# A two-layer diffusion trunk on one core: another order of two modulation sums, and another engine for their first products

## The chip, the cores and the metric

The kernel runs on one core of a Trainium2 chip. The metric is the device time of one execution in microseconds. The kernel before took 1355.4 us (median of three runs, 1355.3 to 1356.14). The profiled execution took 1356.77 us, of which 1355.0 us lie between its first and its last recorded instruction.

## What is computed

Two layers run over 384 tokens (128 context tokens, 256 latent tokens) of width 2048. What matters here is the modulation that each layer draws from two condition vectors (`c_ctx` for context tokens, `c` for latent ones):

```
for layer in range(2):
    m = silu(cond) @ w_mod + b_mod            # cond: c_ctx and c; w_mod 2048 x 6144
    shift, scale, gate = split(m, 3)          # columns 0-2047, 2048-4095, 4096-6143
    h = rmsnorm(x, norm_g) * (1 + scale) + shift
    x = x + gate * mixer(h)                   # mixer: projections, attention, output projection
```

All numbers are float32. The `gate` columns of layer 0 are needed when layer 0's output projection is added to x. The `shift` and `scale` columns of layer 1 are needed when layer 1's input is made out of that sum.

## The kernel before, in words

**The matrix work.** Every projection is cut into groups of 512 output columns (`group`, line 375). A group loads its weights in eight pieces of 512 KB (`w_piece`, line 365) through the DMA queue of SyncE. ScalarE rounds each piece to a short format (`whi`, line 370), VectorE makes the rest (`wlo`, line 372), and TensorE makes three products for each tile. The results stand in PSUM banks with the tag `mm`, of which there are four; a group in the token-major form uses three of them. Three `whi` and two `wlo` buffers exist. Weight pieces are issued with a high priority, everything else in the order in which the program emits it. A scheduler then orders each engine's instructions once, ahead of the run; on the chip each engine and each DMA queue works strictly in that order.

**The modulation sums.** Of layer 0 the scale and shift columns are made by TensorE in the first 215 us (`start_mod`). All others come from eight sums on VectorE, each over 1024 columns of a `w_mod` (`mod_acc`, line 263): for each of 16 row blocks a piece of 512 KB is loaded on SyncE's queue into one of three `mraw` buffers, and for each of the two condition vectors the piece, times a scalar per partition, is added to `acc`. `acc` has one buffer: the next sum can't write it before the sum ahead has been read out. A unit of such a sum is one row block (two instructions). The first row block has no sum yet to add to, and is a plain product (line 284).

**The two ends of a sum.** `mod_part` (line 291) ends with four small TensorE matmuls that add over partitions, a ScalarE copy `ev` (line 300), four transposes, and one or two small VectorE instructions: it gives shift or scale columns of layer 1. `mod_gates` (line 311) first waits, while the program is written, until a flag says that the tiles it writes are free (line 314); its end then broadcasts `b_mod` by DMA on GpSimd's queue, splits `acc` into `ahi` (ScalarE) and `alo` (VectorE) four times, adds over partitions by eight matmuls, and adds the bias four times on VectorE. It gives two groups of gate rows.

**Who decides when.** The sums stand in two lists, `mods` and `rows` (line 336); `unit` (line 338) runs the next unit, `rows` ahead of `mods`, one sum at a time. `pump` (line 348) is called after each weight piece. It runs units while the pace allows and while the planned VectorE time, plus 2.7, stays under the planned TensorE time (lines 350 to 354). Planned times are added up by `cost_v` and `cost_t` (lines 56 to 66) for VectorE and TensorE instructions only; a lead of TensorE beyond 6.0 is dropped. `finish` (line 356) runs units at once until the gate rows that are needed exist. It is called after each group of layer 0's output projection (line 1076), before its three PSUM tiles are multiplied by the gate rows.

**The order of the sums.** `mods` holds layer 1's columns from blocks 16, 24, 0 and 8, and then the first gate rows of layer 0 (line 776). The flag of the latter, `ready0`, is set at line 1032, after the last group but one ahead of the output projection. The gate rows for the third and fourth group go into `rows` after the first group (line 1079). `finish_mods` (line 1084) empties `mods` before the fourth group is used.

Of the kernel before, what the change touches and what calls it, by code (L numbers as in the profile page):

```python
# [10 lines left out]
AF = mybir.ActivationFunctionType  # L11
ALU = mybir.AluOpType
# [33 lines left out]
def trunk_kernel(ctx: ExitStack, tc: tile.TileContext, I, O):  # L46
# [39 lines left out]
    nc = Core()  # L86
# [15 lines left out]
    def nm(s):  # L102
        uid[0] += 1
        return f"{s}_{uid[0]}"

    def px():
        return psx.tile([P, 512], F32, tag="px", name=nm("px"))

    def t6(tag, dt=F32):
        return tpool.tile([P, 1536], dt, tag=f"t{tag}", name=nm(f"t{tag}"))  # L110
# [138 lines left out]
    def mod_cols(l, k0, nk, cp):  # L249

        like = (lambda a: a.rearrange("p (h b) c -> p h b c", h=2)) if len(cp.shape) == 4 else (lambda a: a)
        nc.vector.tensor_tensor(
            out=like(modc[l][:, k0:k0 + nk, :]), in0=cp,
            in1=like(bcol[l][:, k0:k0 + nk].unsqueeze(2).broadcast_to([P, nk, 2])), op=ALU.add)
        if KT <= k0 < 2 * KT:
            q = slice(k0 - KT, k0 - KT + nk)
            nc.vector.scalar_tensor_tensor(
                out=acol[l][:, q, :], in0=modc[l][:, k0:k0 + nk, :], scalar=1.0,
                in1=gcol[l][:, q].unsqueeze(2).broadcast_to([P, nk, 2]), op0=ALU.add, op1=ALU.mult)
# [3 lines left out]
    def mod_acc(l, c0):  # L263

        acc = mpool.tile([P, 2, 1024], F32, tag="acc", name=nm("acc"))
        cs = csil_g[l] if c0 >= 2 * D else csil
        raws = []

        def load(kt):
            raws.append(wpool.tile([P, 1024], F32, tag="mraw", bufs=MRAWB, name=nm("mraw")))  # L270
            nc.sync.dma_start(raws[kt], I[f"l{l}_w_mod"][kt * P:kt * P + P, c0:c0 + 1024])


        for kt in range(MRAWB - 1):
            load(kt)
        yield
        for kt in range(KT):
            if kt + MRAWB <= KT:
                load(kt + MRAWB - 1)
            raw = raws[kt]  # L280
            for c in range(2):
                s = cs[:, kt, c:c + 1]
                if kt == 0:
                    nc.vector.tensor_scalar(out=acc[:, c], in0=raw, scalar1=s, scalar2=None, op0=ALU.mult)
                else:
                    nc.vector.scalar_tensor_tensor(out=acc[:, c], in0=raw, scalar=s, in1=acc[:, c],
                                                   op0=ALU.mult, op1=ALU.add)
            yield
        return acc

    def mod_part(l, k0):

        acc = yield from mod_acc(l, k0 * P)
        ps = px()
        for j in range(4):
            nc.tensor.matmul(ps[32 * j:32 * j + 32, :], lhsT=ones[:, 0:32],
                             rhs=acc[:, j % 2, 512 * (j // 2):512 * (j // 2) + 512], start=True, stop=True)
        ev = mpool.tile([P, 512], F32, tag="t2", bufs=T2B, name=nm("ev"))
        with tc.high_priority(BOOST):
            nc.scalar.copy(ev, ps)  # L300
        for _ in range(EVY):
            yield
        cp = px()
        for b in range(4):
            nc.tensor.transpose(cp[:, b * P:b * P + P], ev[:, b * P:b * P + P], ident)
        mod_cols(l, k0, 8, cp.rearrange("p (b h c r) -> p h b c r", b=4, h=2, c=2)[:, :, :, :, 0])
        yield
# [3 lines left out]
    def mod_gates(l, g0, tags, ready):  # L311

        acc = yield from mod_acc(l, 2 * D + 512 * g0)
        while not ready[0]:
            yield
        for i in range(2):
            c0 = 2 * D + 512 * (g0 + i)
            gb = t6(tags[i])[:, 0:1024].rearrange("p (c n) -> p c n", c=2)
            for c in range(2):
                nc.gpsimd.dma_start(gb[:, c], I[f"l{l}_b_mod"][c0:c0 + 512].partition_broadcast(P))  # L320
            for c in range(2):
                ps = px()
                a = acc[:, c, 512 * i:512 * i + 512]
                hi = mpool.tile([P, 512], F32R, tag="t2", bufs=T2B, name=nm("ahi"))
                nc.scalar.copy(hi, a)
                lo = mpool.tile([P, 512], F32R, tag="t2", bufs=T2B, name=nm("alo"))
                nc.vector.tensor_tensor(out=lo, in0=a, in1=hi.bitcast(F32), op=ALU.subtract)
                nc.tensor.matmul(ps, lhsT=ones_r, rhs=hi, start=True, stop=False)
                nc.tensor.matmul(ps, lhsT=ones_r, rhs=lo, start=False, stop=True)
                nc.vector.tensor_tensor(out=gb[:, c], in0=ps, in1=gb[:, c], op=ALU.add)  # L330
            gates[l, g0 + i] = gb
        yield
# [3 lines left out]
    mods, rows, now = [], [], []  # L336
# [436 lines left out]

    phases = START
    ready0 = [False]
    mods += [mod_part(1, k0) for k0 in (16, 24, 0, 8)] + [mod_gates(0, 0, "KL", ready0)]
    pace[1] = RATE0
    for _ in start_mod(*phases[0]):
        pass
# [452 lines left out]
def _program(shapes):  # L1232
    import concourse.bacc as _bacc

    nc = _bacc.Bacc("TRN2", target_bir_lowering=False, num_devices=1)
    I = {n: nc.dram_tensor(f"in_{n}_dram", s, d, kind="ExternalInput").ap() for n, (s, d) in shapes.items()}
    O = {n: nc.dram_tensor(f"out_{i}_dram", s, F32, kind="ExternalOutput").ap() for i, (n, s) in enumerate(_OUTS)}
    with tile.TileContext(nc) as tc:
        trunk_kernel(tc, I, O)
    return nc  # L1240
# [12 lines left out]
```

## Time and profile before

| | us |
|---|---|
| median of three runs | 1355.4 |
| the profiled execution | 1356.77 |
| its span, first to last instruction | 1355.0 |
| TensorE matmul busy | 1321.0 (97%) |
| VectorE busy | 1019.0 (75%) |
| ScalarE busy | 647.9 (48%) |
| GpSimd busy | 72.4 (5%) |

PE stands for TensorE's matmuls, PEld for its weight loads, DVE for VectorE, ACT for ScalarE, POOL for GpSimd, SP for SyncE. Line 77 is a helper through which every VectorE and TensorE instruction goes, so these are told apart by tile names: `mm` is a result of a weight group, `px` any other PSUM tile, `acc` and `mraw` belong to the modulation sums. Neighbouring matmuls overlap in the records, so that a busy TensorE says that its queue was not waiting, not that it did more than one thing. In the timeline, the number in brackets at the end of a line is how long the engine stood idle before, and what ended that.

### The profile page before, as it was taken

To read this page: it belongs to the slowest core of one execution; us is meant where nothing else is said; L and a number is where in the kernel's file an instruction comes from. 1 tells how busy PE (TensorE), PEld (TensorE's weight loads), DVE (VectorE), ACT (ScalarE), POOL (GpSimd) and SP (SyncE) were. 2 spreads that over 40 slices of the span, in tenths; PEclk is the share of its full clock that TensorE was granted. 3 is DMA by queue.
4 is the path that set the end of the run, shared out by engine and by line. 5 is a ranking of instruction groups with operands and counts; after the bars stand their busy time and mean duration, and the time that the engine had idled before them with its cause. 6 is when DMAs were issued, how large, how long until landed. Compare 5 with 4: busy or idle time off the path is not lost.

```text
span 1355.0 us, 19101 instructions
## 1 busy us (share of the span) xinstructions
PE 1321.0 (97%) x7093; PEld 1125.7 (83%) x7093; DVE 1019.0 (75%) x1602; ACT 647.9 (48%) x1297; POOL 72.4 (5%) x84
## 2 busy tenths in 40 slices
PE   5899999999999999999999999999999999999998
PEld 4678888997888878787987887888888999998887
DVE  5678757998998745896998969995656664499743
ACT  4532233476655534755433347345766763352221
POOL 1000000000000021101000000200000101000000
PEclk8899999999999999999999999999999999999999
DMA  9989989755555334576778854784332345457642
GB/s 284 304 289 331 317 289 319 236 160 179 176 174 181 97 106 138 167 232 201 242 244 254 297 184 133 234 283 119 92 94 81 104 118 166 129 181 254 210 152 84
DMA packets 138317, 265.42 MB, mean 196 GB/s; under 512 B 8944, under 2 KB 46768, under 8 KB 138224
## 3 DMA queue, kind: packets, MB, share of 16 engines
q1 hardware_dynamic: 132592, 246.52, 56.9%
q0 software_dynamic: 5376, 17.60, 4.5%
q8 instruction: 56, 0.92, 0.3%
q14 instruction: 37, 0.30, 0.1%
q10 hardware_dynamic: 256, 0.08, 0.0%
HBM read 256.04 MB, written 8.13 MB: 195 GB/s over the span
## 4 chain that ended last, share of the span: by engine, by line
PE 91%; DMA 4%; DVE 3%; ACT 1%; POOL 1%; issue 0%; DVEq 0%; ACTq 0%; SPq 0%; POOLq 0%
PE mm L77 77%; PE px L77 14%; DMA raw<-in_l_w_in_dram 2%; DMA mraw<-in_l_w_mod_dram 1%; DVE wlo L77 1%; DVE acc L77 1%; DMA tB<-in_x_sample_dram 0%; ACT whi L370 0%; POOL sm L444 0%; DVE tB L77 0%; DMA rowc<-in_c_dram 0%; DVE tG L77 0%; ACT tE L469 0%; DVE tH L77 0%; POOL r L444 0%
## 5 line engine op out<-in xcount | busy, mean ns | idle before, releaser
L370 ACT CAST whi<-raw 128x1024 fp32r<-128x1024 f32 (+1 forms) x270 | 278.4, 1032 | 500.1 <-PE mm L77 393.7
L77 DVE TENSOR_TENSOR wlo<-raw,whi 128x1024 fp32r<-128x1024 f32 (+1 forms) x270 | 323.4, 1198 | 188.0 <-PE mm L77 148.6
L77 PE MATMUL mm<-whi,hh 128*128 128x512 f32 x1008 | 398.9, 396 | 0.0
L77 PE MATMUL mm<-wlo,hh 128*128 128x512 f32 x1008 | 391.7, 391 | 3.2 <-DVE wlo L77 3.2
L77 PE MATMUL mm<-whi,hl 128*128 128x512 f32 x1008 | 393.5, 391 | 0.6 <-DVE hl L77 0.6
L77 DVE SCALAR_TENSOR_TENSOR acc<-mraw,csil,acc 128x1024 f32<-128x1024 f32 x240 | 299.0, 1279 | 9.0 <-DMA mraw<-in_l_w_mod_dram 9.0
L77 PE MATMUL mm<-hh,whi 128*128 128x384 f32 x768 | 264.4, 347 | 7.1 <-ACT hh L471 4.6
L77 PE MATMUL mm<-hl,whi 128*128 128x384 f32 x768 | 259.2, 338 | 0.0
L77 PE MATMUL mm<-hh,wlo 128*128 128x384 f32 x768 | 254.5, 338 | 0.2 <-DVE wlo L77 0.2
L77 PEld LDWEIGHTS mm<-wlo,hh 128*128 128x128 f32 x1008 | 189.3, 188 | 42.7 <-DVE wlo L77 5.8
L77 PEld LDWEIGHTS mm<-whi,hl 128*128 128x128 f32 x1008 | 189.3, 188 | 40.8 <-DVE hl L77 1.5
L77 PEld LDWEIGHTS mm<-whi,hh 128*128 128x128 f32 x1008 | 189.4, 188 | 39.3 <-ACT tE L824 0.8
L77 PEld LDWEIGHTS mm<-hh,whi 128*128 128x128 f32 x768 | 145.3, 190 | 22.2 <-issue 10.1
L77 PEld LDWEIGHTS mm<-hh,wlo 128*128 128x128 f32 x768 | 144.8, 189 | 2.7 <-DVE wlo L77 1.0
L77 PEld LDWEIGHTS mm<-hl,whi 128*128 128x128 f32 x768 | 145.5, 190 | 1.2 <-issue 0.2
L623 ACT ACTIVATE p<-px,nb,rs 128x384 f32<-128x384 f32 (+1 forms) x72 | 42.4, 596 | 15.0 <-DVE nb L77 14.5
L77 PE MATMUL px<-mraw,cs 128*32 128x256 f32 (+1 forms) x576 | 40.4, 377 | 4.9 <-DMA mraw<-in_l_w_mod_dram 4.9
L633 ACT ACTIVATE p<-p,sum 128x384 f32<-128x384 f32 (+1 forms) x72 | 36.1, 540 | 15.1 <-DVE sum L77 13.2
L77 DVE TENSOR_REDUCE mx<-px 128x1 f32<-128x384 f32 (+1 forms) x54 | 29.7, 567 | 9.3 <-PE px L77 8.9
L77 PEld LDWEIGHTS px<-mraw,cs 128*32 128x32 f32 x576 | 16.3, 114 | 20.0 <-issue 8.2
L77 PEld LDWEIGHTS px<-ct,p 128*128 128x128 f32 x168 | 20.1, 141 | 8.3 <-issue 2.8
L444 POOL TENSOR_TENSOR rs<-rs,nhalf 128x12 f32<-128x12 f32 x6 | 14.7, 2450 | 227.5 <-DVE rs L77 227.5
(415 smaller groups left out, 1228.5 us busy)
## 6 DMA issues: line engine op xcount, KB each, us to landing
raw<-in_l_w_in_dram SPq DMA_DIRECT2D x194, 512.0 KB, 3.9
mraw<-in_l_w_mod_dram SPq DMA_DIRECT2D x192, 512.0 KB, 5.0
raw<-in_l_w_out_dram SPq DMA_DIRECT2D x64, 512.0 KB, 4.9
raw<-in_l_w_in_dram SPq DMA_DIRECT2D x12, 256.0 KB, 6.6
tK<-in_l_b_mod_dram POOLq DMA_DIRECT2D x6, 256.0 KB, 6.0
y1d<-tA POOLq DMA_DIRECT2D x2, 768.0 KB, 5.2
tD<-y1d POOLq DMA_DIRECT2D x2, 768.0 KB, 6.0
tL<-y1d POOLq DMA_DIRECT2D x2, 768.0 KB, 6.2
```

Source lines behind the costliest of these rows:

```text
L77: return f(*a, **k)
L370: nc.scalar.copy(hi, raw)
L444: nc.gpsimd.tensor_tensor(out=out, in0=out, in1=nhalf[:, 0:out.shape[1]], op=ALU.pow)
L623: nc.scalar.activation(p[:, j], ss[j], AF.Exp, bias=nb[:, j:j + 1], scale=rs[:, i + j:i + j + 1], accum_out=sm[:, j:j + 1])
L633: nc.scalar.activation(p[:, j], p[:, j], AF.Copy, scale=sm[:, j:j + 1])
```

## The change

```
 mod_acc, line 281:
             for c in range(2):
                 s = cs[:, kt, c:c + 1]
                 if kt == 0:
-                    nc.vector.tensor_scalar(out=acc[:, c], in0=raw, scalar1=s, scalar2=None, op0=ALU.mult)
+                    nc.scalar.activation(acc[:, c], raw, AF.Copy, scale=s)
                 else:
                     nc.vector.scalar_tensor_tensor(out=acc[:, c], in0=raw, scalar=s, in1=acc[:, c],
                                                    op0=ALU.mult, op1=ALU.add)

 line 773:
     phases = START
     ready0 = [False]
-    mods += [mod_part(1, k0) for k0 in (16, 24, 0, 8)] + [mod_gates(0, 0, "KL", ready0)]
+    mods += [mod_part(1, k0) for k0 in (16, 24, 0)] + [mod_gates(0, 0, "KL", ready0), mod_part(1, 8)]
     pace[1] = RATE0
```

In each of the eight sums the two plain products of the first row block go from VectorE to ScalarE. ScalarE instructions are not in the planned times. And the sum for layer 0's first gate rows stands ahead of that for the last quarter of layer 1's shift columns.

## Rows read from the trace of the kernel before

**Rows 1.** The page: busy us and share of the span, by engine.
```profile
PE 1321.0 (97%) x7093; PEld 1125.7 (83%) x7093; DVE 1019.0 (75%) x1602; ACT 647.9 (48%) x1297; POOL 72.4 (5%) x84
```
**Rows 2.** The page: the chain that ended last, by engine.
```profile
PE 91%; DMA 4%; DVE 3%; ACT 1%; POOL 1%; issue 0%; DVEq 0%; ACTq 0%; SPq 0%; POOLq 0%
```
**Rows 3.** Timeline of PE: start, length, instruction, idle before it and releaser.
```profile
501.42 0.50 PE L77 MATMUL mm<-wlo,hh 128*128 128x512 f32 x1 [1.39 <-DVE wlo L77]
...
636.92 0.66 PE L77 MATMUL px<-ct,ev 128*128 128x128 f32 x4 [0.71 <-ACT ev L300]
...
734.50 0.50 PE L77 MATMUL mm<-wlo,hh 128*128 128x512 f32 x1 [1.50 <-DVE wlo L77]
...
739.23 0.50 PE L77 MATMUL mm<-wlo,hh 128*128 128x512 f32 x1 [0.33 <-DVE wlo L77]
...
832.75 0.50 PE L77 MATMUL mm<-whi,hl 128*128 128x512 f32 x1 [0.21 <-DVE hl L77]
```
**Rows 4.** Stretches: busy us (count) of PE, PEld, DVE, ACT, POOL; clock, DMA, GB/s.
```profile
640.00:660.00 20.00, 20.00 (x126) 19.94 (x125) 19.68 (x22) 7.84 (x13) 1.80 (x3) 1.00 0.74 244
...
700.00:720.00 20.00, 20.00 (x93) 15.96 (x92) 18.89 (x25) 8.29 (x13) 1.60 (x3) 1.00 0.75 214
720.00:740.00 20.00, 18.17 (x80) 14.42 (x79) 15.89 (x14) 7.92 (x15) 1.49 (x3) 1.00 0.87 287
740.00:760.00 20.00, 19.72 (x93) 16.10 (x92) 20.00 (x21) 8.72 (x18) 2.02 (x3) 1.00 0.82 264
760.00:780.00 20.00, 20.00 (x89) 16.25 (x88) 18.86 (x17) 4.85 (x6) 0.00 (x0) 1.00 0.93 330
780.00:800.00 20.00, 20.00 (x95) 15.88 (x94) 16.96 (x32) 11.34 (x22) 1.33 (x2) 1.00 0.66 217
```
**Rows 5.** Tile acc: its instructions, ns min/median/max, first and last start.
```profile
L77 DVE SCALAR_TENSOR_TENSOR acc<-mraw,csil,acc x240: 1257/1279/1293, 36.0 to 1265.0; 128x1024 f32<-128x1024 f32 x120
...
L77 PE MATMUL px<-acc,ct x32: 592/592/617, 194.9 to 635.6; 128*32 128x512 f32 x32
L77 DVE TENSOR_SCALAR acc<-mraw,csil x16: 742/750/936, 34.7 to 1198.0; 128x1024 f32<-128x1024 f32 x16
...
L77 DVE TENSOR_TENSOR alo<-acc,ahi x16: 680/684/693, 707.0 to 1316.9; 128x512 fp32r<-128x512 f32 x16
```
**Rows 6.** Timeline of DVE at 34, 719, 732 and 784 us.
```profile
34.66 1.41 DVE L77 TENSOR_SCALAR acc<-mraw,csil 128x1024 f32<-128x1024 f32 x2
...
719.09 0.75 DVE L77 TENSOR_SCALAR acc<-mraw,csil 128x1024 f32<-128x1024 f32 x1
...
732.03 1.29 DVE L77 SCALAR_TENSOR_TENSOR acc<-mraw,csil,acc 128x1024 f32<-128x1024 f32 x1 [4.11 <-DMA mraw<-in_l_w_mod_dram]
...
784.62 0.69 DVE L77 TENSOR_TENSOR tA<-mm,tK 128x512 f32<-128x512 f32 x1
```
**Rows 7.** The chain in order of time, its piece at 728 us.
```profile
727.95 7.86 DMA mraw<-in_l_w_mod_dram
```
**Rows 8.** Stretch of 3 us, columns as in Rows 4.
```profile
730.00:733.00 3.00, 3.00 (x14) 2.15 (x12) 0.97 (x1) 0.19 (x1) 0.00 (x0) 1.00 1.02 401
```
**Rows 9.** Timeline of POOL: the bias broadcasts of the first gate rows.
```profile
619.11 1.06 POOL L320 DMA_DIRECT2D tL<-in_l_b_mod_dram  x2 [25.15 <-PE px L77]
```
**Rows 10.** Timeline of ACT at 32, 41, 649, 668 and 728 us.
```profile
32.75 1.79 ACT L736 COPY tA<-mm 128x384 f32<-128x384 f32 x4 [2.03 <-PE mm L77]
...
41.83 1.63 ACT L736 COPY tD<-mm 128x384 f32<-128x384 f32 x4 [2.67 <-PE mm L77]
...
649.29 1.99 ACT L497 ACTIVATE hh<-px,onh 128x384 fp32r<-128x384 f32 x4
...
668.60 1.75 ACT L494 CAST hh<-tA 128x384 fp32r<-128x384 f32 x4
...
728.73 1.05 ACT L370 CAST whi<-raw 128x1024 fp32r<-128x1024 f32 x1 [3.02 <-PE mm L77]
```
**Rows 11.** Timeline of DVE at 827 us: the seventh sum's first product.
```profile
827.42 0.74 DVE L77 TENSOR_SCALAR acc<-mraw,csil 128x1024 f32<-128x1024 f32 x1
```

More of the change, by code (lines that the diff above doesn't have):

```diff
@@ L283, in mod_acc @@
                 if kt == 0:
-                    nc.vector.tensor_scalar(out=acc[:, c], in0=raw, scalar1=s, scalar2=None, op0=ALU.mult)
+                    nc.scalar.activation(acc[:, c], raw, AF.Copy, scale=s)
                 else:
@@ L775, in trunk_kernel @@
     ready0 = [False]
-    mods += [mod_part(1, k0) for k0 in (16, 24, 0, 8)] + [mod_gates(0, 0, "KL", ready0)]
+    mods += [mod_part(1, k0) for k0 in (16, 24, 0)] + [mod_gates(0, 0, "KL", ready0), mod_part(1, 8)]
     pace[1] = RATE0
```

## The prediction

> **What bounds the kernel now.** I read the busy shares first, then the chain of waits, then TensorE's own idle stretches in the timeline, and last the stretches around the edit. TensorE is busy for 1321.0 of 1355.0 us, VectorE for 1019.0, ScalarE for 647.9 [rows 1], and 91% of the chain that ended last lies on TensorE [rows 2]. So a microsecond taken off another engine counts only where TensorE was waiting for that engine. After 220 us the timeline shows nine such waits, of 1.39, 0.71, 1.50, 0.33, 0.28, 0.65, 0.38, 0.22 and 0.21 us, 5.7 us in all ([rows 3] has the first, the last and the three that matter here). The other 28 of the 34 us without matmul lie in the first 220 us and behind the last matmul. From 640 us to the end of layer 0's output projection VectorE is nearly full, 19.68, 18.89, 15.89, 20.00 and 18.86 us of 20 in the rows shown [rows 4]: here the modulation sums fill all of its time that the weight pieces leave. This is also where both edits bite.
>
> **The change, part by part.**
>
> **1. The order of two sums.** Nothing is added or removed: 32 instructions on VectorE, 16 loads of 512 KB on SyncE's queue and an end for each sum, in the other order. I followed the pump's own clocks (lines 350 to 358, prices of lines 56 to 66) by hand through both orders, to see only which unit is written where. Before, the layer-1 sum ends just ahead of `ready0`, the gate sum runs through the next two weight groups, and `finish` after the first output group finds one row block and the whole end still to do; both are rushed in front of the three multiplications that free PSUM. After, the gate sum is complete before `ready0` and waits there (some four empty units), its end follows at once with the first piece of the next group, and the layer-1 sum runs through the two groups. It is then some two row blocks short at the first output group, where nothing is rushed any more; it ends in the second group, and the gate sum for groups three and four follows. At the third group `finish` finds the same two row blocks and the same end as before. The bias broadcasts that the moved end issues on GpSimd's queue were already out by 619.11 us before [rows 9], so that queue sees little of it.
>
> What it takes off the path. (a) The wait of 0.71 us at 636.92 [rows 3] is for the copy `ev` of the layer-1 sum's end, which stood alone between two weight groups. After, this end stands inside the second output group, among matmuls. The other three ends of this kind show no TensorE wait. I take -0.71; bounds -0.71 and 0. (b) The waits of 1.50 and 0.33 us [rows 3] come from a `wlo` that stood behind a row block of the next gate sum, which waited 4.11 us for its load [rows 6]; the chain shows that load taking 7.86 us [rows 7]. That sum had only just begun there, behind the rushed end (its first product at 719.09, [rows 6]), while the output write, the next residual tiles and weight pieces were in flight too. After, a sum in its steady rhythm stands there. I take -1.83; bounds -1.83 and 0, since the DMA engines are full at this place (share 1.02, 401 GB/s, [rows 8]) with or without the rush.
>
> What it may add. After 640 us VectorE has no room to catch up, and the third group's rows are due at about 784.62, the first product with them [rows 6], with TensorE not stalled there (20.00 of 20, [rows 4]). The instructions due by then are nearly the same, but two changes of sum now stand in between, and `acc` has one buffer. At the first the layer-1 sum must let the gate end read `acc`: eight VectorE instructions of 0.684 us or about that [rows 5], some 5.5 us, which before came 60 us later. At the second it waits for four matmuls of 0.592 us [rows 5] that overlap in part, and then for ScalarE's pair. I put what VectorE leaves idle at these two places at 2.5 and 3 us, half of each chain and a little. Against it stand the 4.11 us of load wait that go, and two pairs of plain products, each 1.41 us [rows 6], of which about 2.8 us. The sum is 5.5 - 4.1 - 2.8 = -1.4 us, a little early; if the load wait stays and the idle doubles it is 11 - 2.8 = 8.2 us late. TensorE has a free fourth bank and two buffered pieces, some 3 us of work at the pace of 90 matmuls in 20 us that 760 to 780 shows [rows 4]. So the cost runs from 0 to about 5 us; I take +0.5, near the lower end because the sum is negative.
>
> **2. The first products on ScalarE.** VectorE loses 16 instructions of 0.750 us [rows 5], 12.0 us. ScalarE gets 16 in their place. The nearest rows: a cast of the same 128x1024 takes 1.05 us; four instructions of 384 columns with a scalar per partition take 1.99 us, four casts 1.75 [rows 10], so the scalar costs 0.06 us. That is 1.05 to 1.11 us each, 16.8 to 17.8 us in all, 647.9 to about 665. I take 1.1, and 2.2 for a pair. What hides it: ScalarE is less than half used in every stretch of [rows 4] but one, and the weight cast there stood 3.02 us idle ahead of it [rows 10], since it waits for TensorE to free a buffer. A pair fits in such a gap. Where it doesn't, the cast behind it waits, then `wlo`, then TensorE: the price without cover is up to 2.2 us a sum, and more where the product itself waits for its load or for `acc`. What waits behind it on VectorE is the second row block alone.
>
> The Trainium skill ("ScalarE: Activation LUTs", sections "What ACT_TABLE_LOAD costs" and "Rules for kernel authors") tells against this edit: a multiplication belongs on VectorE, and an ACTIVATE with one per-partition operand costs 0.279 us + 0.833 ns a column. For 1024 columns that is an estimate of 1.13 us, against the 1.11 bounded above; the sum by it would be 18.1 us on ScalarE, 0.3 more, and nothing else changes. Were ScalarE's time on the path, as that rule takes it, 16 products at 0.38 us more than VectorE's 0.75 would cost 6.1 us, which is about the fourth rival below; the gaps in the rows are why it gets a small chance.
>
> Place by place: the first pair falls at 34.66 [rows 6], where VectorE did it with no wait. ScalarE has idle stretches of 2.03 and 2.67 us there, but between them it drains PSUM for TensorE without a pause [rows 10], and the stage is bound by DMA. If the pair lands ahead of those copies, and its load is late, TensorE pays 0 to 2.2 us and the wait; I take +0.5, a quarter, since either gap would hold it. Six of the other seven fall where TensorE had no wait: 0, the gap of 3.02 us being the cover. The seventh falls at 827.42 [rows 11], in the chain that starts layer 1: -0.7 if VectorE's time there was on the path, +1.1 if ScalarE's is; I take 0. Nothing is left of the planner's saving of 1.32 a sum: its lead is cut to 6.0 within a pump or two at most of these places, so units move by one step in the third and fourth sum only.
>
> **The sum:** -0.71 - 1.83 + 0.5 + 0.5 + 0 = -1.54 us on a span of 1355.0. The profiled execution took 1356.77, 1.77 more than its span and 1.37 more than the median; what lies around the span doesn't change, so the difference goes onto the median: 1355.4 - 1.5 = **1353.9 us**. I call a change measurable here beyond 0.2%, 2.7 us: below 1352.7 or above 1358.1. The forecast is a small gain inside that.
>
> **The rivals.**
>
> *The load wait stays* (16%). The DMA share of 1.02 is for it: the write, the residual tiles and the weight pieces meet there whatever sum runs. Against it: one group later, 740 to 760, VectorE is full, the share is 0.82 [rows 4], and of TensorE's nine waits only that of 0.28 lies there, apart from the tail of this one. Then 1355.4 - 0.71 + 1.0 = 1355.7.
>
> *More comes free* (22%). Every engine's order is computed anew from 34 us on, VectorE has 12 us more, and the nine waits and some of the 28 us outside them can shrink with it. For it: VectorE is the engine that the longest of these waits name. Against it: most of the first stage's waits are for loads and ScalarE. The other waits near the edit and at 820 us, some 1.5 us, and 1 to 2 us of the first stage: 1353.9 - 3 = 1351.
>
> *The third group's rows come late* (14%), the other side. Mechanism: `acc` is one buffer, VectorE is full from 640 on, and the gate sum for groups three and four can't start before the layer-1 sum has been read out, where before it began at 719. If it is more than the 3 us of TensorE's cover late at 784, TensorE stops until the rows are there; from 5.5 us late on this eats the gain and more. At the 8.2 us above it costs 5, and the load wait has stayed: 1355.4 - 0.71 + 0.5 + 5.2 = 1360.4; halfway 1358.3.
>
> *ScalarE's queue holds the weight casts* (7%). It is strictly in order; a product that waits for its load or for `acc` holds the next cast. For it: VectorE waited for such loads. Against it: the first load of a sum is issued early. At four of eight places for 1.5 us, and the rest as forecast: 1353.9 + 6 = 1359.9.
>
> **How the numbers follow.** The forecast's own case has 41%, own range 1352.4 to 1355.4; with the load wait 57% lie between 1352 and 1356. Faster by over 0.2%: 22% and a sixth of the forecast's 41, 29%. Slower by over 0.2%: the last two, 21%. Within: 50%. The range takes in the free case at 1351 with a microsecond, and the late rows as far as halfway: 1350.2 to 1358.6.
>
> **What would show it.** Right on step 1: no `px<-ahi` matmul near 709 us but near 645; no TensorE wait at 636 and none above 1 us between 700 and 745; the four `px<-acc` of the last layer-1 sum near 730. Right on step 2: 16 ScalarE instructions `acc<-mraw` of 1.0 to 1.1 us, VectorE's busy time near 1007, ScalarE's near 665, and no cast that waits longer for it. Wrong: a TensorE wait of 2 us or more between 782 and 795 that names VectorE (late rows), waits on `whi` where a sum begins (ScalarE's queue), a first stage that ends more than 1 us later, or a time beyond the range on either side.

## The result, and the profile after

The changed kernel takes 1363.26 us in the median of 4 runs (1362.11 to 1364.98), the kernel before 1355.77 beside it (1355.3 to 1357.85): a ratio of 1.0053, 95% interval 1.0036 to 1.0071. Forecast were 1353.9 us and a range that ended at 1358.6. The change costs 7.5 us, and the prediction was wrong in size and in sign. The profiled execution took 1363.62 us with a span of 1361.9.

The page's busy line answers to [rows 1]: VectorE has 10.0 us less, ScalarE 16.0 more, TensorE 3.5 more.

```profile
PE 1324.5 (97%) x7093; PEld 1127.8 (83%) x7093; DVE 1009.0 (74%) x1586; ACT 663.9 (49%) x1313; POOL 70.6 (5%) x84
```

TensorE's timeline between 600 and 800 us (start, length, instruction, idle before it and releaser) answers to [rows 3]:

```profile
684.79 0.50 PE L77 MATMUL mm<-whi,hh 128*128 128x512 f32 x1 [2.04 <-DVE gt L77]
...
787.43 0.67 PE L77 MATMUL mm<-wlo,hh 128*128 128x512 f32 x1 [2.49 <-DVE wlo L77]
...
791.37 0.50 PE L77 MATMUL px<-ahi,ones_r 128*128 128x512 f32 x1 [0.19 <-ACT ahi L325]
...
792.56 0.49 PE L77 MATMUL px<-alo,ones_r 128*128 128x512 f32 x1 [0.69 <-DVE alo L77]
...
793.26 0.50 PE L77 MATMUL px<-ahi,ones_r 128*128 128x512 f32 x1 [0.21 <-ACT ahi L325]
```

The waits at 636.92, 734.50 and 739.23 are gone, as forecast. Two places that had no wait have 5.62 us of them: the gate stage at 684, and the start of the third output group at 787.

The stretches of the kernel after (busy us and count of PE, PEld, DVE, ACT, POOL; then granted clock, DMA share, GB/s) answer to [rows 4]; the 2-us rows show what follows each of the two long waits:

```profile
620.00:640.00 20.00, 19.98 (x104) 16.65 (x103) 8.89 (x15) 11.41 (x23) 2.56 (x5) 1.00 0.56 158
...
640.00:660.00 20.00, 20.00 (x122) 19.05 (x120) 15.80 (x19) 10.75 (x15) 1.80 (x3) 1.00 0.57 184
...
680.00:700.00 20.00, 17.96 (x73) 14.34 (x72) 18.58 (x22) 6.88 (x10) 0.00 (x0) 0.91 0.64 209
...
720.00:740.00 20.00, 20.00 (x95) 15.63 (x94) 11.63 (x12) 8.07 (x11) 0.00 (x0) 1.00 0.85 286
...
780.00:800.00 20.00, 16.42 (x62) 11.95 (x61) 18.88 (x24) 5.36 (x8) 0.58 (x1) 0.91 0.62 205
...
684.00:686.00 2.00, 1.21 (x4) 0.97 (x5) 2.00 (x5) 0.62 (x2) 0.00 (x0) 0.80 0.64 227
686.00:688.00 2.00, 2.00 (x6) 1.58 (x5) 1.13 (x2) 1.20 (x3) 0.00 (x0) 0.50 0.00 0
688.00:690.00 2.00, 2.00 (x9) 1.58 (x8) 1.45 (x3) 1.05 (x2) 0.00 (x0) 0.85 0.24 57
...
788.00:790.00 2.00, 2.00 (x6) 1.56 (x5) 2.00 (x3) 0.62 (x1) 0.00 (x0) 0.50 0.77 262
```

Three things are to be seen. VectorE is less busy at 640 (15.80 against 19.68 us) and at 720 (11.63 against 15.89), the two places where one sum follows another. TensorE loses its time later, at 680 and 780. And after each long wait the granted clock falls to 0.50, its level of 1.2 GHz: a 2-us row then holds 6 matmuls instead of 10 or 11, though TensorE shows as busy.

How much each place costs can be counted between the same matmuls, those of the product `mm` that have the same number in both traces (numbers from the starts in the two timelines, the place named by its time before):

| from, to (before) | us before | us after | difference | of it waits |
|---|---|---|---|---|
| 600.0 to 652.1 | 52.0 | 52.2 | +0.2 | -0.7 |
| 675.1 to 690.1 | 15.0 | 18.9 | +3.9 | +2.0 |
| 705.0 to 735.1 | 30.1 | 27.7 | -2.3 | -1.5 |
| 735.1 to 780.1 | 45.0 | 43.7 | -1.3 | -0.6 |
| 780.1 to 800.2 | 20.1 | 26.2 | +6.1 | +3.6 |

The stretches between don't differ by 0.1. The sum is +6.6; the last matmul starts 6.9 us later, and the two profiled executions differ by 6.85. In the second and the last row the matmuls are the same in number (67 and 93), so the 1.9 and 2.5 us beyond the waits are slower matmuls: the clock. In the rows between them the end of the gate sum has moved out and that of the layer-1 sum in.

Now the reason, on VectorE. Two rows of the kernel before that the prediction did not read (stretches ahead of [rows 4]):

```profile
600.00:620.00 20.00, 19.99 (x104) 17.05 (x103) 19.36 (x32) 13.09 (x29) 0.89 (x2) 1.00 0.78 243
620.00:640.00 20.00, 19.29 (x105) 15.22 (x104) 7.70 (x13) 10.94 (x22) 1.98 (x4) 1.00 0.63 196
```

VectorE has a hole there already: 7.70 busy of 20 us. The sum has been added up and the next can't start, since `acc` is read only where the sum's end stands in the engines' order. The tile `acc` on VectorE between 604 and 622 us shows when the last row block was done (count; min, median, max ns; first and last start), before:

```profile
L77 DVE SCALAR_TENSOR_TENSOR acc<-mraw,csil,acc x7: 1270/1276/1284, 606.0 to 616.9; 128x1024 f32<-128x1024 f32 x7
```

and after:

```profile
L77 DVE SCALAR_TENSOR_TENSOR acc<-mraw,csil,acc x3: 1267/1284/1284, 606.2 to 608.6; 128x1024 f32<-128x1024 f32 x3
```

After, the pause runs from 608.6 to the pair that opens the next sum, on ScalarE at 649.73; before, from 616.9 to the first product at 636.28: 41 us against 19. Not all of the difference is the order's doing: with the products off VectorE the sum is also added up sooner (kernels 1 and 2 below tell the two apart). The timeline of VectorE before has the opening, and the `alo` that begins the third group's rows:

```profile
636.28 1.42 DVE L77 TENSOR_SCALAR acc<-mraw,csil 128x1024 f32<-128x1024 f32 x2 [0.40 <-PE px L77]
...
781.59 0.68 DVE L77 TENSOR_TENSOR alo<-acc,ahi 128x512 fp32r<-128x512 f32 x1
```

The timeline of ScalarE after has both openings, each pair 2.19 us, and between them the tanh of the gate stage, which waits 4.91 us for VectorE:

```profile
649.73 2.19 ACT L284 ACTIVATE acc<-mraw,csil 128x1024 f32<-128x1024 f32 x2
...
682.64 0.49 ACT L680 ACTIVATE gt<-mm 128x384 f32<-128x384 f32 x1 [4.91 <-DVE tB L77]
...
732.67 2.19 ACT L284 ACTIVATE acc<-mraw,csil 128x1024 f32<-128x1024 f32 x2
```

And the timeline of VectorE after shows the debt being paid at 676 and 782:

```profile
642.92 1.22 DVE L77 TENSOR_TENSOR wlo<-raw,whi 128x1024 fp32r<-128x1024 f32 x1 [4.18 <-PE mm L77]
...
676.14 1.28 DVE L77 SCALAR_TENSOR_TENSOR acc<-mraw,csil,acc 128x1024 f32<-128x1024 f32 x1
677.34 1.22 DVE L77 TENSOR_TENSOR wlo<-raw,whi 128x1024 fp32r<-128x1024 f32 x1
678.47 3.67 DVE L77 SCALAR_TENSOR_TENSOR acc<-mraw,csil,acc 128x1024 f32<-128x1024 f32 x3
682.06 1.02 DVE L77 TENSOR_TENSOR tB<-tB,gt 128x384 f32<-128x384 f32 x2
...
733.72 0.17 DVE L77 TENSOR_TENSOR modc<-px,par 128x16 f32<-128x16 f32 x1 [1.50 <-PE px L77]
...
782.57 3.67 DVE L77 SCALAR_TENSOR_TENSOR acc<-mraw,csil,acc 128x1024 f32<-128x1024 f32 x3
786.15 1.22 DVE L77 TENSOR_TENSOR wlo<-raw,whi 128x1024 fp32r<-128x1024 f32 x1
787.29 2.47 DVE L77 SCALAR_TENSOR_TENSOR acc<-mraw,csil,acc 128x1024 f32<-128x1024 f32 x2
789.68 0.68 DVE L77 TENSOR_TENSOR alo<-acc,ahi 128x512 fp32r<-128x512 f32 x1
```

In VectorE's order, row blocks that found no place in the hole now stand ahead of urgent work: three of their instructions ahead of the gate product at 682.06, for which ScalarE's tanh and then TensorE wait, and three ahead of the `wlo` at 786.15, for which TensorE waits 2.49 us. The third group's first `alo` comes at 789.68; before it came at 781.59.

### The profile page after: what moved, and what is told of

Same layout as the page of the kernel before. It is cut to its first block, busy times and chain, and to the rows that moved or that the text cites. A ratio compares the mean times of both kernels' runs of the same rounds, so it can differ in the third digit from the quotient of the medians.

```text
span 1361.9 us, 19109 instructions
## 1 busy us (share of the span) xinstructions
PE 1324.5 (97%) x7093; PEld 1127.8 (83%) x7093; DVE 1009.0 (74%) x1586; ACT 663.9 (49%) x1313; POOL 70.6 (5%) x84
## 4 chain that ended last, share of the span: by engine, by line
PE 90%; DVE 4%; DMA 3%; issue 1%; ACT 1%; POOL 1%; ACTq 0%; DVEq 0%; SPq 0%; POOLq 0%
PE mm L77 76%; PE px L77 14%; DVE acc L77 2%; DMA mraw<-in_l_w_mod_dram 2%; DVE wlo L77 1%; DMA tC<-in_x_sample_dram 1%; DMA raw<-in_l_w_in_dram 0%; DVE tB L77 0%; DMA rowa<-in_l_norm_dram 0%; POOL sm L444 0%; ACT whi L370 0%; DVE hl L77 0%; DVE tG L77 0%; ACT tE L469 0%; DVE tH L77 0%
```

## The experiments

Theory A: the new order lengthens the pause between two sums that share the single `acc`; VectorE falls behind, and TensorE pays at 684 and 787, in waits and in clock. Rival B: ScalarE's queue, with the first products in it, holds weight casts. The other rivals are in the expectations. Every ratio is to the kernel before on the same chip, in five rounds of timing; its medians were 1355.99 (first four experiments), 1356.58 (next four), 1356.01 (next three) and 1356.83 (the last).

| kernel | order | first products | own accumulator | us | ratio, 95% interval |
|---|---|---|---|---|---|
| 1 | new | VectorE | no | 1362.22 | 1.0046 (1.0033 to 1.0060) |
| 2 | old | ScalarE | no | 1353.97 | 0.9985 (0.9973 to 0.9997) |
| 3 | new | ScalarE | layer-1 sum | 1355.23 | 0.9996 (0.9987 to 1.0005) |
| 4, gate product first | new | ScalarE | no | 1357.86 | 1.0013 (1.0001 to 1.0024) |
| 5, gate rows of groups 3, 4 ahead too | newer | ScalarE | no | 1356.88 | 1.0000 (0.9987 to 1.0013) |
| 6, gate product first | new | ScalarE | layer-1 sum | 1356.02 | 1.0000 (0.9989 to 1.0010) |
| 7 | old | ScalarE | layer-1 sum | 1388.85 | 1.0241 (1.0224 to 1.0257) |
| 8 | new | VectorE | layer-1 sum | 1355.26 | 0.9995 (0.9985 to 1.0005) |
| 9 | old | ScalarE | gate sum | 1351.00 | 0.9960 (0.9944 to 0.9975) |
| 10, gate product first | old | ScalarE | no | 1355.13 | 0.9984 (0.9972 to 0.9995) |
| 11, as 2 | old | ScalarE | no | 1354.36 | 0.9987 (0.9975 to 0.9999) |
| 12 | old | VectorE | gate sum | 1355.07 | 0.9985 (0.9973 to 0.9996) |

**1 and 2: each half alone.** 1 is the changed kernel with

```diff
-                    nc.scalar.activation(acc[:, c], raw, AF.Copy, scale=s)
+                    nc.vector.tensor_scalar(out=acc[:, c], in0=raw, scalar1=s, scalar2=None, op0=ALU.mult)
```

and 2 the changed kernel with the old order.

> The changed kernel with the first products back on VectorE: only the order of the two sums differs from before. Theory A (the order: with one acc buffer the layer-1 sum waits for the end of the gate sum, and the gate sum for groups three and four waits for the end of the layer-1 sum; VectorE has nothing to do meanwhile, the rows of group three come late, TensorE stops and its clock drops): 1362 to 1366 us, as the change or a little above, with TensorE waits of 2 us or more near 684 and 787 us. Rival B (the products on ScalarE hold the weight casts): within 2 us of before, about 1355. Rival C (a reshuffled schedule, both halves contribute): about 1359.

> The kernel before with the first products on ScalarE, the order of the sums as before. Theory A: no loss, 1353 to 1356 us, since VectorE gets 12 us off and ScalarE has room; TensorE's waits of 1.50 and 0.33 us near 734 stay or shrink. Rival B: 1360 us or more, with waits on whi where a sum begins. Rival C: about 1359.

The order alone costs 6.2 us; ScalarE's products alone take off 2.0. That refutes B and puts the loss on the order. The timeline of TensorE in 1 names the same two places, with single waits below the 2 us that theory A expected (the third group has five, 3.06 us in all). At the first place two instructions of row blocks stand ahead of the gate product, against three in the changed kernel; that one more (1.28 us) is about the 1.20 us by which its wait is longer.

```profile
685.13 0.50 PE L77 MATMUL mm<-whi,hh 128*128 128x512 f32 x1 [0.84 <-DVE gt L77]
...
784.85 0.50 PE L77 MATMUL mm<-wlo,hh 128*128 128x512 f32 x1 [1.34 <-DVE wlo L77]
```

The pause at the first change of sum is 33 us in 1, from 619.0 to 652.37 on VectorE, and 24 in 2, from 607.6 to 631.43 on ScalarE (for each the tile `acc` on VectorE between 604 and 622 us, then the opening):

```profile
L77 DVE SCALAR_TENSOR_TENSOR acc<-mraw,csil,acc x9: 1268/1278/1283, 603.5 to 619.0; 128x1024 f32<-128x1024 f32 x9
...
652.37 1.41 DVE L77 TENSOR_SCALAR acc<-mraw,csil 128x1024 f32<-128x1024 f32 x2
```

```profile
L77 DVE SCALAR_TENSOR_TENSOR acc<-mraw,csil,acc x3: 1268/1281/1281, 605.1 to 607.6; 128x1024 f32<-128x1024 f32 x3
...
631.43 1.15 ACT L284 ACTIVATE acc<-mraw,csil 128x1024 f32<-128x1024 f32 x1
```

So the length of the pause alone doesn't price it: 2 has a longer one than the kernel before and is no slower. What counts is how much of the sums is left undone behind it. The instructions that add or open a row block, counted up to the same matmul of the product `mm` (named by its time before):

| up to | before | changed | 1 | 2 | 3 |
|---|---|---|---|---|---|
| 600.0 | 118 | 123 | 118 | 123 | 123 |
| 652.1 | 136 | 132 | 131 | 138 | 144 |
| 735.1 | 168 | 165 | 165 | 170 | 180 |
| 780.1 | 192 | 187 | 188 | 192 | 192 |

With either engine for the products the new order is five or six instructions short at 652.1 (1 against the kernel before, the changed kernel against 2). A part of that is the gate sum's end, which stands earlier in the new order; but at 735.1, where both ends are done in either order, three and five are still missing, and at 780.1 four and five, each 1.28 us of VectorE. Kernel 3 comes next.

**3: the changed kernel, the layer-1 sum with an accumulator of its own.** The buffer is that of layer 0's `kT`, last read near 620 us.

```diff
-    def mod_acc(l, c0):
+    def mod_acc(l, c0, own=False):
...
+        if own:
+            acc = apool.tile([P, 4, 512], F32, tag="kT", name=nm("acc")).rearrange("p (c a) n -> p c (a n)", c=2)
+        else:
             acc = mpool.tile([P, 2, 1024], F32, tag="acc", name=nm("acc"))
...
-        acc = yield from mod_acc(l, k0 * P)
+        acc = yield from mod_acc(l, k0 * P, (l, k0) == (1, 8))
```

> The changed kernel, where the last layer-1 sum gets an accumulator of its own (a buffer of the same size that stands empty between the two layers' attention), so that neither it nor the gate sum behind it waits for acc. Theory A: the two VectorE gaps (4.2 us idle in 640 to 660, 8.4 in 720 to 740) shrink to about 3 us together, no TensorE wait over 1 us near 684 or 787, no stretch at half clock there: 1353 to 1357 us. Rival B: no change, 1362 to 1364. Rival C: anything, about 1360.

The order is the new one, and the loss against the kernel before is gone. Its stretches, columns as above:

```profile
620.00:640.00 20.00, 19.98 (x107) 17.28 (x106) 19.02 (x26) 14.40 (x28) 2.87 (x5) 1.00 0.84 262
...
780.00:800.00 20.00, 20.00 (x94) 16.02 (x93) 14.87 (x30) 10.39 (x21) 1.33 (x2) 1.00 0.49 154
```

VectorE fills the hole, 19.02 us in place of 8.89, and nothing stops TensorE at 780. This is the direct evidence for A: sums, their order in the program and products are the same, and only the buffer differs.

**4 and 5: one of the two places each.** 4 is the changed kernel with

```diff
-            nc.vector.tensor_tensor(out=o[:, h], in0=o[:, h], in1=G, op=ALU.mult)
+            with tc.high_priority(BOOST):
+                nc.vector.tensor_tensor(out=o[:, h], in0=o[:, h], in1=G, op=ALU.mult)
```

> The changed kernel with the gate product of gate_heads (line 1021) given the priority of the eviction ahead of it, so that row blocks of a sum can't stand between the two. Theory A: the wait of 2.04 us at 684.79 and the stretch at half clock behind it go, 3.5 to 4 us, the wait at 787 stays: 1358.5 to 1360.5 us. A rival to this piece of A: the same row blocks are only pushed back and the third group's rows come later by as much, so that 787 grows: 1362 to 1364.

The wait at 684 is gone, that at the third group stays, and the clock still falls (TensorE's timeline, then the stretch):

```profile
779.77 0.50 PE L77 MATMUL mm<-wlo,hh 128*128 128x512 f32 x1 [1.39 <-DVE wlo L77]
```

```profile
786.00:788.00 2.00, 2.00 (x6) 1.60 (x5) 1.68 (x3) 0.62 (x1) 0.02 (x1) 0.50 0.00 0
```

5 does the opposite; the layer-1 sum comes last.

```diff
-    mods += [mod_part(1, k0) for k0 in (16, 24, 0)] + [mod_gates(0, 0, "KL", ready0), mod_part(1, 8)]
+    ready2 = [False]
+    mods += [mod_part(1, k0) for k0 in (16, 24, 0)] + [mod_gates(0, 0, "KL", ready0), mod_gates(0, 2, "KM", ready2),
+                                                      mod_part(1, 8)]
...
-            rows.append(mod_gates(0, 2, "KM", ready0))
+            ready2[0] = True
```

> The changed kernel, with the gate rows of the third and fourth group summed ahead of the last quarter of layer 1's columns too; that quarter comes last. Theory A (the changed order makes VectorE idle where one sum follows another on the single acc buffer, and the third group's rows are then late): those rows are now two row blocks or more ahead of their use, so no TensorE wait above 0.7 us stands between 775 and 800 and the granted clock there is 1.00; the first change of sum at 640 to 650 is the same, so the wait for the gate instruction at 684 may stay. 1356 to 1358.5. Rival D (the reorder costs because any sum moved within this full stretch of VectorE lands late wherever it is due): the last quarter is then late at its own use behind 820, and the time is 1361 or more.

The wait at 684 stays as it was, with its fall of the clock, and the third group's rows are in time:

```profile
684.01 0.50 PE L77 MATMUL mm<-whi,hh 128*128 128x512 f32 x1 [2.03 <-DVE gt L77]
```

```profile
780.00:800.00 20.00, 19.55 (x91) 15.74 (x91) 20.00 (x24) 9.19 (x19) 1.33 (x2) 1.00 0.89 305
```

Each against the kernel before beside it, the changed kernel is 7.5 us slower, 4 is 1.9 slower, 5 is 0.3 slower and 3 is 0.8 faster: mending one place gives 5.6 or 7.2 us, mending both 8.3. The traces don't show that one mend takes anything from the other: between the matmuls of 780.1 and 800.2 kernel 4 loses 6.2 us, as the changed kernel does, so its rows were not pushed back further, and between those of 675.1 and 690.1 kernel 5 loses 3.9. 4 came out a little faster than theory A expected; the changed kernel's interval is almost 5 us wide, too wide to tell by the medians whether the two mends add up.

**6 and 8: whether more is to be had in the new order.** 6 is 3 with the gate product first, 8 is 3 with the products on VectorE.

> The changed kernel with the last quarter's own accumulator and the gate product at boosted priority, so both repairs at once. Theory A: the own accumulator alone left no TensorE wait above 0.65 us between 640 and 830, so the boost finds nothing left to remove: 1354.3 to 1356, the same as with the accumulator alone (1355.2). If the two losses were independent, with the gate product still hurting somewhere, it comes out 2 us or more lower: 1353 or less.

> The new order with the last quarter's own accumulator, all first products on VectorE: with the other three (before, order alone, order with accumulator and ScalarE's products) this closes a square. Theory A: the accumulator gives back what the order cost whether or not ScalarE makes the products: 1354.5 to 1357, no TensorE wait above 0.7 us between 775 and 800. Rival B' (it takes both, VectorE's 12 us less work and the accumulator): 1358 to 1361, with waits for wlo or gt left at 684 or 787.

Both come out as 3 did. With its own buffer the new order is level with the kernel before, whoever makes the products. (It is not level with the old order that has such a buffer too; see behind 12.)

**7: the old order with the same buffer for the layer-1 sum.**

> The order of before, the first products on ScalarE, and the last quarter of layer 1's columns with an accumulator of its own. Theory A (one acc buffer is what makes a change of sum cost, in either order): with before's order the end that read acc at 636 no longer holds the next sum's first product, and VectorE is ahead from there on: 1352.5 to 1354, at or a little below the order of before with ScalarE's products alone (1354.0). Rival F (the own accumulator repaired the new order only, since before's order has its sums' changes where TensorE has cover): 1354 within 0.7 and the same waits at 748 and 768 as without it.

A miss, and of the experiment's making: in the old order this sum starts before 600 us, while `kT` is read until 616.6. Its first row block comes at 618, and TensorE's order has the sum's end where it was (timeline, then stretches):

```profile
661.55 3.03 PE L77 MATMUL px<-acc,ct 128*32 128x512 f32 x8 [28.77 <-DVE acc L77]
```

```profile
664.00:668.00 4.00, 2.98 (x13) 2.00 (x10) 3.06 (x4) 2.78 (x6) 0.00 (x0) 0.50 0.76 245
...
672.00:674.00 2.00, 2.00 (x8) 1.22 (x7) 0.95 (x1) 0.53 (x2) 0.01 (x1) 0.75 0.68 231
674.00:676.00 2.00, 2.00 (x13) 2.00 (x12) 1.52 (x4) 0.83 (x3) 1.79 (x3) 1.00 0.30 88
```

It says nothing on A or F, but it shows what a late end costs when TensorE has nothing else in front: the whole lateness, 28.8 us, and 10 us at a granted clock of 0.50 behind it.

**9 to 12: the old order, with the buffer for the sum that starts when it is free.** 9 is 2 with the `own` of 3 given to the gate sum:

```diff
-        acc = yield from mod_acc(l, 2 * D + 512 * g0)
+        acc = yield from mod_acc(l, 2 * D + 512 * g0, (l, g0) == (0, 0))
```

10 is 2 with the gate product first, 11 is 2 again, 12 is 9 with the products on VectorE.

> The order of before, the first products on ScalarE, and the own accumulator given to the gate sum of the first two groups, which starts behind 620 us, when the buffer is free in any case. Theory A (a single acc buffer costs VectorE at every change of sum): the change at 636 and the one near 720 no longer wait for the sum ahead to be read out, VectorE runs further ahead, and the waits of 1.0 us at 748 to 750 and 0.35 at 768 go or shrink: 1352 to 1353.5, 0.5 to 1.5 us below the order of before with ScalarE's products alone. Rival F (in before's order TensorE has cover at the changes of sum, so nothing is to be had there): the same as that kernel within 0.7 us.

> The order of before, the first products on ScalarE, and the gate product of the output projection at boosted priority. Theory A: the gate's place among VectorE's instructions costs only where VectorE is behind, which it isn't in before's order: the same as without the boost, 1353.5 to 1355. If the gate product costs at each of the four groups in any order, 1 us or more comes off: 1353 or less.

> The order of before with the first products on ScalarE, a second time and on the same chip as the two kernels beside it, since its gain of 0.15% stood close to what can be told from nothing. Theory A: 0.997 to 0.9995 of before again. If it was chance: 0.9995 to 1.001.

> The order of before, all first products on VectorE, and the gate sum of the first two groups with an accumulator of its own: the kernel before with that single edit. Theory A (in before's order too the single acc buffer costs, and VectorE's 12 us of products cost beside it): it takes off about what it took off beside ScalarE's products, 1.5 to 3.5 us, so 1352.5 to 1354.5, and the waits of 0.71 at 636 and 1.50 at 734 are gone. Rival G (the accumulator helps only with ScalarE's products, since VectorE has no time to run ahead without them): 1355 to 1356.5.

9 beats both kernels: 1351.0 us in 7 runs (1350.38 to 1355.35), 0.4% below the kernel before. Its stretches:

```profile
620.00:640.00 20.00, 19.98 (x106) 15.52 (x105) 19.84 (x25) 11.53 (x23) 1.92 (x4) 1.00 0.90 302
...
760.00:780.00 20.00, 20.00 (x89) 16.14 (x88) 8.20 (x9) 6.41 (x7) 0.00 (x0) 1.00 0.47 144
```

The hole is filled (19.84), and by 760 VectorE has time to spare (8.20 in place of the 18.86 of [rows 4]); from 700 to 800 TensorE has no wait. The hole in the kernel before was thus worth something too: alone the buffer takes off 1.8 us (12), the products 2.0 and 1.65 (2 and 11), both together 5.0. That is more than their sum, but the intervals reach over that. F is refuted: 9 stands 3.4 us below the same kernel without the buffer (11), more than A expected. The gate product first (10) is worth nothing where VectorE isn't behind.

12 doesn't part A from G cleanly. The 1.8 us are what A expected to come off and its interval ends just below 1, against G; but the kernel before was at 1356.83 beside it, so that 1355.07 itself lies in G's range. The wait of 1.50 is gone, that of 0.71 is not, against A:

```profile
639.16 0.66 PE L77 MATMUL px<-ct,ev 128*128 128x128 f32 x4 [0.71 <-ACT ev L303]
```

The buffer doesn't take all of the new order's price. With ScalarE's products and a buffer of its own for the sum that opens at the first change, the old order is at 0.9960 (9) and the new at 0.9996 (3), with intervals apart: some 4 us. With VectorE's products it is 0.9985 (12) and 0.9995 (8), too close to tell. Between the matmuls of 735.1 and 780.1 the trace of 3 has 1.45 us of TensorE waits, that of 9 none. What the rest is was not tested.

## Why the prediction was wrong

**Step 1, (a) and (b)** held: no wait at 636, none at 734 and 739, and -1.83 and -0.71 as taken. One reading in (b) was wrong: the load of 7.86 us [rows 7] ran from 727.95 to 735.81, so it can't be the one that the row block of 732.03 had waited for; it stands in the chain ahead of the wait of 0.33 at 739.23. The order of the units, worked out by hand, was right as well: the layer-1 sum ends in the second group (its `ev` just ahead of 732.67), and at the third group row blocks and the whole end are left.

**Step 1, "What it may add"** failed; it is the term of +0.5 us. It measured +6.1 at the third group and +3.9 at the gate stage. Three things went wrong in it.

First, VectorE's lateness, summed up as 5.5 - 4.1 - 2.8 = -1.4. Between the same matmuls, 600.0 to 652.1, VectorE stands idle for 12.9 us before, 15.5 in kernel 1 and 20.3 in the changed kernel; from 705.0 to 735.1, where the load wait of 4.11 went, for 5.2, 4.5 and 8.5. So for the order alone (kernel 1) the two changes of sum add 2.6 and 3.4 us, close to my 2.5 and 3. Wrong was what I set against them. The relief of 2.8 us can't be used in the new order: what the products free is spent in front of the shut `acc`, where 7.4 us of idle time are added in place of 2.6, and 5 instructions ahead of the kernel before at 600.0 become 4 behind at 652.1. And I left the due time where it was, though (a) and (b) bring TensorE there sooner: from the matmul of 600.0 to that of 780.1 kernel 1 takes 2.5 us less than the kernel before. Its 1.9 us of added idle time (2.6 + 3.4 - 4.1) and these 2.5 make 4.4 us late, beyond the 3 us of cover. "Waits there (some four empty units)" was in my own text, but I priced empty units at nothing. I read the stretches from 640 on; the row at 620, with 7.70, would have shown that work stands still there already.

Second, the cover. The forecast had the third group's rows 1.4 us early; the first `alo` came 8.1 us later than before, 781.59 to 789.68, with TensorE about 1 us later. That is the case of 8.2 us that the rival "the third group's rows come late" had worked out, with its mechanism, at 5.2 us for TensorE, and its sign was the right one: "a TensorE wait of 2 us or more between 782 and 795 that names VectorE" is the 2.49 at 787. I gave it 14%, since I held my own sum of -1.4 for the likely one. Its time, 1360.4, is 2.9 us low. (Its "halfway 1358.3" doesn't follow from its terms: halfway between 1355.4 - 0.71 + 0.5 and 1360.4 is 1357.8.)

Third, what no case had: the stall at 684, where row blocks stood ahead of the gate product, and the clock. Of the 10.0 us lost at the two places 4.4 are matmuls at a lower clock. A wait was priced as its length; here it cost nearly twice that.

**Step 2** held in its sizes. A pair takes 2.19 us, forecast 2.2; VectorE has 1009.0 us, ScalarE 663.9, forecast 1007 and about 665. One alone takes a little over the 1.1 taken (tile `acc` on ScalarE, after):

```profile
L284 ACT ACTIVATE acc<-mraw,csil x16: 1132/1151/1212, 38.7 to 1202.6; 128x1024 f32<-128x1024 f32 x16
```

The Trainium skill ("ScalarE: Activation LUTs", "What ACT_TABLE_LOAD costs") makes it 1.13 us by its formula, and the trace agrees. Its table "Rules for kernel authors" puts a multiplication on VectorE. In the old order kernels 2 and 11 came out the other way: a product costs more on ScalarE (1.15 us against 0.75), and the kernel gains. That VectorE is nearly full there while ScalarE has room is the likely reason; no run varied it by itself.

The rest of step 2, taken as 0, was a gain of about 2 us in the old order: part of the rival "more comes free". In the new order nothing of it is seen (1.0046 without the products, 1.0053 with them, intervals overlapping). In the traces the difference lies at 684: 0.84 us of wait without the products on ScalarE, 2.04 with them and the fall of the clock behind it, one more instruction of a row block being ahead of the gate product. Why VectorE's order has one more there is not settled. The +0.5 for the start can't be told either. At 215 us the changed kernel stands 0.5 us behind before, but kernels 2 and 11, the same program twice, stand there 2.0 and 0.4 us ahead of it, and at 222 us 0.5 ahead and 2.4 behind: the granted clock falls to 0.50 in between, in 11 for longer. No run had the first pair alone on VectorE.

## What to carry to other kernels

Work that fills an engine's gaps needs a place to go in every gap: with one accumulator, the time from the last addition to the last read is lost to it. A reorder is priced by how much of the backlog is still undone behind that time, counted up to the same place of the bottleneck engine, and not by the instructions that it moves; and where the reorder also speeds that engine up, the due times come sooner. So read the stretches ahead of the edit too, and look for an engine that stands idle while its backlog is due later. And look at the granted clock behind a wait of TensorE before the wait is priced.

## What was not expected of the hardware

The granted clock falls after quite short waits. After one of 2.04 us (684) it stands at 0.50 within 2 us of the restart and is back at 1.00 by 690; the same in kernel 5 after 2.03. In kernel 4 it fell behind five waits of 1.39, 0.19, 0.64, 0.20 and 0.68 us between 779 and 785. After single waits of 1.50 (before, at 734) and 0.84 us (kernel 1, at 685) it stayed at 1.00. At 0.50, matmuls of 512 columns start 0.43 us apart (686.35, 686.78, 687.21 in the timeline after) instead of 0.23.
